# Chunk scores of a bidirectional SSD mixer: masked CB triangles kept in PSUM, time-step weights formed ahead of the exponentials

## The chip, the cores and the metric

The kernel runs on one core of a Trainium2 chip. The metric is device time in microseconds (us) of one execution, as the median of several runs; lower is better. The core's engines are called by the profile's names: PE (TensorE; PEld is its weight load), DVE (VectorE), ACT (ScalarE), POOL (GpSimd) and SP (which only issues DMAs here). A program on one core works out of SBUF and of PSUM, which has eight banks of 128 partitions x 512 float32.

## The reference, cut to what matters

One encoder block on 1024 tokens plus 16 meta tokens, width 1024: an input projection, a gated depthwise convolution, a bidirectional Mamba-2 (SSD) mixer with 4 groups of 8 heads, a gated merge, and a SwiGLU feed-forward part. The change lies in the SSD mixer. It works in chunks of 128 tokens. For a chunk and a direction:

```python
cb = jnp.einsum('bclgn,bcsgn->bcgls', cc, bc)          # one 128x128 matrix per group
lmat = jnp.exp(segsum(adt))                            # one triangle of decays per head
y_diag = jnp.einsum('bcgels,bcsgep->bclgep', cb[:, :, :, None] * lmat, xdt)   # xdt = x * dt
```

So each head's product needs CB, cut to a triangle (lower for the forward direction, upper for the backward one), times the exponentials, times the head's time steps dt. The kernel adds both directions before the product with x.

## The kernel before, in words

The work comes in stages. First an input projection with float32 operands split into a high and a low part, so each product is three matmuls. Then the two convolutions, on DVE with help from ACT and POOL. Then the SSD stage, where the change is. Then the merge and the feed-forward part, which are nearly all matmuls.

**The SSD stage.** Lines 871 to 901 write the order of work out by hand. `backward(0)` runs first: 27 steps that transpose x and B and carry the backward state of group 0. After that a loop visits 32 chunks (4 groups x 8). In each round it walks the string `SEQ` (line 41): `L` loads the next chunk (`load`, line 763), `s` and `t` build its masked decays for heads 0 to 3 and 4 to 7 on POOL (`select`, line 784, instruction on line 760), `S` and `T` turn them into weights (`scores`, line 792), `D`, `O`, `C`, `M`, `V` make the current chunk's outputs, state and norm, and `b`/`e` take a step of the next group's `backward`. The digits are places where background matmuls are let in.

**The background.** `background()` (line 642) is other matmul work that needs no DVE of its own: the two gates' projections (32 groups of 24 matmuls, line 548) and the first half of the SSM output product (16 such groups, line 652). A group accumulates in one PSUM bank with the tag `mm`; ACT copies the bank to SBUF (lines 557 and 658), and a DMA stores it. It is a generator that stops after 6, 15 and 24 matmuls of each group. `step_bg(n)` (line 667) adds `n` to a running sum and takes a step for each whole 1; the weights in `BGW` (line 42) sum to 3.3 for a round.

**Order on the engines.** From line 665 to 902 each matmul is tied behind the one before it, so PE's order is the program's. The other engines' order comes from the framework's scheduler, which sorts ready instructions by program order at build time; each engine then runs its list strictly in that order.

**PSUM.** Line 592 gives the eight banks out as `mm` 2, `tp` 2, `yo` 2, `ss` 1, `yd` 1. After the stage, `ps_ring` (line 593) passes six of them in turn to the later matmuls.

**The weights of a chunk.** `load` computes CB with one matmul into a `tp` bank (line 776), and DVE multiplies it by the two masks into two SBUF tiles, `cbf` (line 778) and `cbb` (line 780). `scores(h4)` adds up the decays on PE into the `ss` bank, ACT takes the exponentials into `e` (line 798), and then, for each of four heads, ACT writes `cbf * dt_f` into `gg` (line 802) and DVE adds `cbb * dt_b` (line 803):

```python
S.activation(out=gg[0][:, h], in_=self.cbf, func=AF.Copy, scale=dt[...])
V.scalar_tensor_tensor(out=gg[0][:, h], in0=self.cbb, scalar=dt[...], in1=gg[0][:, h], op0=ALU.mult, op1=ALU.add)
```

Then DVE multiplies `e` by `gg` (line 805). In the next round `outputs` uses `e` for the `yd` matmuls (line 825), whose result DVE adds to the skip term (line 829). `split_small` (line 691) splits the C matrix on ACT (693) and DVE (694).

Of the kernel before, what the change touches and what calls it, by code (L numbers as in the profile page):

```python
# [8 lines left out]
F32 = mybir.dt.float32  # L9
F32R = mybir.dt.float32r  # L10
AF = mybir.ActivationFunctionType
ALU = mybir.AluOpType
# [3 lines left out]
P = 128  # L16
# [6 lines left out]
NCH = NTT + 1  # L23
DI = 2048
G = 4
HG = 8
# [15 lines left out]
BGW = (0.15, 0.46, 0.29, 0.58, 1.05, 0.14, 0.62, 0.01)  # L42
BG0, BGI = 1.1, 4
ENG = dict(xw="g", xd="v", yy="g", ysz="v", sd="g")
BUFS = dict(xw=4, cc=3, vt=2, s_bl=2, gg=2, e=2, xt=2, btf=5)
LOA, LOB, LOC, LOD = "gg", "vv", "gv", "gv"
EPS = 1e-6
O_VAL, O_GATE, O_Z, O_XS, O_B, O_C, O_DT, O_GC, O_GS = 0, 1024, 2048, 4096, 6144, 6656, 7168, 7232, 8256
# [4 lines left out]
def chunk_span(c):  # L53
    return (0, NM) if c == 0 else (NM + (c - 1) * P, P)
# [3 lines left out]
def tile_hybrid_block(  # L58
# [7 lines left out]
    V, S, GP, PE, SP = nc.vector, nc.scalar, nc.gpsimd, nc.tensor, nc.sync  # L66
    x = x[0]
    out = out[0]
# [126 lines left out]
    def matmul(out_, **kw):  # L195
        tie(PE.matmul(out_, **kw))  # L196

    def transpose(out_, in_, ident_):
        tie(PE.transpose(out_, in_, ident_))  # L199
# [82 lines left out]
    dt = sc.tile([P, NCH, 2 * NH], F32, name="dt")  # L282
# [306 lines left out]

    psB_ctx.close()  # L590
    psp = ctx.enter_context(tc.tile_pool(name="psp", bufs=1, space=PSUM))
    PSB = dict(mm=2, tp=2, yo=2, ss=1, yd=1)
    ps_ring = cycle(("mm", "yo", "ss", "mm", "yo", "yd"))

    def pb(tag):
        return psp.tile([P, 512], F32, name=tag, tag=tag, bufs=PSB[tag])

    def pc():
        return pb(next(ps_ring))

    sd_ctx = ExitStack()
    sd = sd_ctx.enter_context(tc.tile_pool(name="sd", bufs=2))
# [56 lines left out]
            SP.dma_start(out=d_p[i, :, hh * 512:(hh + 1) * 512], in_=pt)  # L659
            yield  # L660

    ps_bg = lambda: pb("mm")
    bg = background()
    bg_acc = [0.0]
    strict[0] = True
# [1 line left out]
    def step_bg(n):  # L667
        bg_acc[0] += n
        while bg_acc[0] >= 1:
            bg_acc[0] -= 1  # L670
            next(bg, None)

    def hbc(t, c, h0, nh, n, w):

        return t[:n, c, h0:h0 + nh].unsqueeze(2).broadcast_to([n, nh, w])
# [3 lines left out]
    def scaled_x(xt, c, h0, n):  # L679
        xw = sd.tile([P, CG], F32, name="xw", bufs=BUFS["xw"])  # L680
        (GP if ENG["xw"] == "g" else V).tensor_tensor(out=v3(xw[:n]), in0=v3(xt[:n]), in1=hbc(wd, c, h0, HG, n, HD), op=ALU.mult)
        return xw
# [8 lines left out]
    def split_small(t):  # L691
        h, l = (sd.tile([P, P], F32R, name=n_, bufs=BUFS["cc"]) for n_ in ("cch", "ccl"))
        S.copy(out=h, in_=t)
        V.tensor_tensor(out=l, in0=t, in1=h.bitcast(F32), op=ALU.subtract)
        return h, l
# [12 lines left out]
    def backward(g):  # L708

        hb = NH + g * HG  # L710
        s_b = None
        for c in range(NCH - 1, -1, -1):
            t0, n = chunk_span(c)
            xc = sd.tile([P, 4, P], F32, name="xc", bufs=3)
            SP.dma_start(out=xc[:, :, :n], in_=d_x[g][:, :, t0:t0 + n])
            bc = sd.tile([P, P], F32, name="bc")
            SP.dma_start(out=bc[:, :n], in_=d_b[g][:, t0:t0 + n])
            ps = pb("tp")
            for j in range(4):
                transpose(ps[:n, j * P:(j + 1) * P], xc[:, j, :n], ident)  # L720
            xt = sd.tile([P, CG], F32, name="xt", bufs=BUFS["xt"])
            S.copy(out=xt[:n], in_=ps[:n])
            SP.dma_start(out=d_xt[g][c, :n], in_=xt[:n])
            yield
            ps = pb("tp")
            transpose(ps[:n, :P], bc[:, :n], ident)
            bt = sd.tile([P, P], F32, name="bt", bufs=BUFS["btf"])
            S.copy(out=bt[:n], in_=ps[:n, :P])
            SP.dma_start(out=d_bt[g][c, :n], in_=bt[:n])
            if c >= 2:  # L730
                xw = scaled_x(xt, c, hb, n)
            yield
            if c >= 2:
                s_b = state_step(s_b, bt, xw, c, hb, n, "s_b")
                SP.dma_start(out=d_sb[g][c - 1], in_=s_b)
            yield
# [3 lines left out]
    def first_state(g):  # L740

        xt = sd.tile([P, CG], F32, name="xt", bufs=BUFS["xt"])
        SP.dma_start(out=xt[:NM], in_=d_xt[g][0, :NM])
        bt = sd.tile([P, P], F32, name="bt", bufs=BUFS["btf"])
        SP.dma_start(out=bt[:NM], in_=d_bt[g][0, :NM])
        xw = scaled_x(xt, 0, g * HG, NM)

        def go():
            state[g] = state_step(None, bt, xw, 0, g * HG, NM, "s_f")
        return go  # L750

    class Chunk:
# [10 lines left out]
        def load(self):  # L763
            g, c = self.g, self.c
            self.first = first_state(g) if c == 1 else None
            t0 = chunk_span(c)[0]
            self.xt = sd.tile([P, CG], F32, name="xt", bufs=BUFS["xt"])
            SP.dma_start(out=self.xt, in_=d_xt[g][c])
            self.bt = sd.tile([P, P], F32, name="bt", bufs=BUFS["btf"])
            SP.dma_start(out=self.bt, in_=d_bt[g][c])  # L770
            bc = sd.tile([P, P], F32, name="bc")
            SP.dma_start(out=bc, in_=d_b[g][:, t0:t0 + P])
            self.cc = sd.tile([P, P], F32, name="cc", bufs=3)
            SP.dma_start(out=self.cc, in_=d_c[g][:, t0:t0 + P])
            ps = pb("tp")
            matmul(ps[:, :P], lhsT=bc, rhs=self.cc, start=True, stop=True)
            self.cbf = sd.tile([P, P], F32, name="cbf")
            V.tensor_tensor(out=self.cbf, in0=ps[:, :P], in1=m_le.bitcast(F32), op=ALU.mult)
            self.cbb = sd.tile([P, P], F32, name="cbb")
            V.tensor_tensor(out=self.cbb, in0=ps[:, :P], in1=m_ge.bitcast(F32), op=ALU.mult)  # L780
            self.e = []
            self.ccs = split_small(self.cc)

        def select(self, h4):
            self.sels = []
            for src in (adh, adl):
                for back in (0, 1):
                    s_ = sd.tile([P, 4, P], F32R, name="sel", bufs=4)
                    self.sel(s_, src.bitcast(F32), (self.hb if back else self.hf) + h4, back)
                    self.sels.append(s_)  # L790

        def scores(self, h4):
            ss = pb("ss")
            for q_, s_ in enumerate(self.sels):
                matmul(ss, lhsT=(u_gt, u_lt)[q_ % 2], rhs=s_.rearrange("p h l -> p (h l)"),
                          start=(q_ == 0), stop=(q_ == 3))
            e = sd.tile([P, 4, P], F32, name="e", bufs=BUFS["e"])
            S.activation(out=e.rearrange("p h l -> p (h l)"), in_=ss, func=AF.Exp)
            gg = [sd.tile([P, 4, P], F32, name="gg", bufs=BUFS["gg"])]
            for h in range(4):  # L800
                hs_ = slice(h4 + h, h4 + h + 1)
                S.activation(out=gg[0][:, h], in_=self.cbf, func=AF.Copy, scale=dt[:, self.c, self.hf:self.hf + HG][:, hs_])  # L802
                V.scalar_tensor_tensor(out=gg[0][:, h], in0=self.cbb, scalar=dt[:, self.c, self.hb:self.hb + HG][:, hs_],  # L803
                                       in1=gg[0][:, h], op0=ALU.mult, op1=ALU.add)
            V.tensor_tensor(out=e, in0=e, in1=gg[0], op=ALU.mult)
            self.e.append(e)

        def outputs(self):
# [60 lines left out]
            SP.dma_start(out=d_vn[g][:, :, i * P:(i + 1) * P], in_=vt)  # L869

    step_bg(BGI)
    for _ in backward(0):
        step_bg(BG0)
    chunks = [Chunk(g, c) for g in range(G) for c in range(1, NCH)]
    NCK = len(chunks)
# [7 lines left out]
    for f in range(NCK + 1):  # L883
        cur = chunks[f] if f < NCK else None
        nxt = chunks[f + 1] if f + 1 < NCK else None
        old = chunks[f - 1] if f else None
        if f % NTT == 0:
            nb = backward(f // NTT + 1) if f // NTT + 1 < G else iter(())
        ahead = lambda: next(nb, None)
        extra = ahead if f % NTT < 2 else (lambda: None)  # L890
        work = dict(
            L=lambda: nxt and nxt.load(), s=lambda: nxt and nxt.select(0), S=lambda: nxt and nxt.scores(0),
            t=lambda: nxt and nxt.select(4), T=lambda: nxt and nxt.scores(4),
            D=lambda: cur and cur.outputs(), O=lambda: cur and cur.off_diag(), C=lambda: cur and cur.carry(),
            M=lambda: cur and cur.norm(), V=lambda: old and old.store(), b=ahead, e=extra)
        for k in SEQ:
            if k in work:
                work[k]()
            else:
                step_bg(BGW[int(k)])  # L900
    step_bg(1000)
    strict[0] = False
    sd_ctx.close()
# [75 lines left out]
    op = load_vn(1)  # L979
# [9 lines left out]
    op = ln_split(0) + ln_split(1)  # L989
# [44 lines left out]
    for b in range(4):  # L1034
        wh, wl = next_w(f"o{b}")
        for i in range(NTT):
            ps = pc()
# [131 lines left out]
```

## Time and profile before

| | |
|---|---|
| median of 3 runs | 2341.51 us (2341.08 to 2342.58) |
| the profiled execution, its own time | 2346.3 us |
| its span, first to last instruction | 2344.1 us |
| PE busy | 2247.3 us (96%) |
| DVE busy | 1445.8 us (62%) |
| ACT busy | 769.1 us (33%) |
| POOL busy | 843.4 us (36%) |
| mean granted TensorE clock | 0.983 of full |

Shares of the whole span mix stages with different limits, so the stage of the change is read alone: it begins with the first score weights at about 785 us of the span, and its last chunk's weights are done at about 1295 us. A matmul's duration in the rows is that of a pipelined instruction: successive matmuls of 512 columns begin 0.23 us apart while each row says 0.39 us. Rows of DVE and ACT overlap by about 0.1 us in the same way.

### The profile page before, as it was taken

Reading aid. Unit: us, or ns where it says so; the run is one execution under the profiler, and the core shown is the slowest. Engines: PE = TensorE matmul, PEld = TensorE weight load, DVE = VectorE, ACT = ScalarE, POOL = GpSimd, SP = SyncE. Lnnn points to the kernel's source line nnn. Section 1 sums busy time; section 2 is a strip of 40 time slices with the busy share of each in tenths; the row PEclk is TensorE's granted clock in tenths of the full one; section 3 lists DMA queues with packets and bytes.
Section 4 is the critical chain, followed back from the end, with each engine's and each line's share of the span. In section 5 each row is a group of like instructions: output and inputs, shape, how many; then the busy total and the mean of one; then the engine's idle time right before and its main releaser. Section 6 shows DMA issues by size and latency. Waiting matters only on the chain.

```text
span 2344.1 us, 31010 instructions
## 1 busy us (share of the span) xinstructions
PE 2247.3 (96%) x12103; PEld 1916.5 (82%) x12103; DVE 1445.8 (62%) x1726; ACT 769.1 (33%) x1385; POOL 843.4 (36%) x730
## 2 busy tenths in 40 slices
PE   8999899999999999888898999999999999999998
PEld 7999899999997666666666778898888888888887
DVE  4398898996771688888999675524233333333236
ACT  6333332323322445445544454214211111111112
POOL 3374654822112576777676241011101101101012
PEclk9999999999999999999999999999999999999999
DMA  4221222233236665656653652421111111111111
GB/s 137 87 72 64 73 76 69 82 104 104 89 102 200 186 198 155 201 155 194 210 167 120 227 177 90 146 66 37 43 47 54 37 54 54 36 54 54 36 54 72
DMA packets 223161, 245.29 MB, mean 105 GB/s; under 512 B 19112, under 2 KB 174360, under 8 KB 223016
## 3 DMA queue, kind: packets, MB, share of 16 engines
q1 hardware_dynamic: 210200, 221.89, 30.6%
q10 hardware_dynamic: 12816, 21.44, 2.5%
q8 instruction: 95, 1.56, 0.3%
q14 instruction: 50, 0.41, 0.1%
HBM read 174.23 MB, written 69.04 MB: 104 GB/s over the span
## 4 chain that ended last, share of the span: by engine, by line
PE 74%; DVE 7%; POOL 6%; issue 4%; DMA 3%; ACT 3%; SPq 0%; POOLq 0%; DVEq 0%; ACTq 0%
PE mm L196 31%; PE yo L196 12%; PE mm L272 6%; PE ss L196 5%; PE yd L196 4%; PE mm L1093 3%; PE yo L1093 3%; DVE gg L803 2%; POOL tap L517 2%; PE ss L1093 2%; PE yd L1093 2%; PE mm L1044 1%; PE yo L1044 1%; POOL wl L139 1%; PE tp L199 1%
## 5 line engine op out<-in xcount | busy, mean ns | idle before, releaser
L139 POOL TENSOR_TENSOR wl<-wraw,wh 128x1024 fp32r<-128x1024 f32 (+1 forms) x103 | 249.9, 2436 | 1116.5 <-ACT wh L138 1116.3
L196 PE MATMUL mm<-hnh,wh 128*128 128x352 f32 (+4 forms) x1248 | 428.0, 343 | 1.4 <-ACT w L275 0.9
L196 PE MATMUL mm<-hnl,wh 128*128 128x352 f32 (+4 forms) x1248 | 421.1, 337 | 0.4 <-DVE hnl L378 0.4
L196 PE MATMUL mm<-hnh,wl 128*128 128x352 f32 (+4 forms) x1248 | 418.7, 335 | 0.0
L138 ACT CAST wh<-wraw 128x1024 fp32r<-128x1024 f32 (+1 forms) x172 | 174.5, 1041 | 403.1 <-PE yd L1093 175.5
L139 DVE TENSOR_TENSOR wl<-wraw,wh 128x1024 fp32r<-128x1024 f32 x69 | 134.4, 1952 | 252.2 <-ACT wh L138 246.5
L478 DVE SCALAR_TENSOR_TENSOR acc<-ap,pr,acc 128x1024 f32<-128x1024 f32 x192 | 247.5, 1289 | 6.3
L196 PEld LDWEIGHTS mm<-hnh,wh 128*128 128x128 f32 x1248 | 235.7, 189 | 15.4 <-issue 2.4
L196 PEld LDWEIGHTS mm<-hnl,wh 128*128 128x128 f32 x1248 | 235.5, 189 | 12.4 <-issue 2.4
L196 PEld LDWEIGHTS mm<-hnh,wl 128*128 128x128 f32 x1248 | 235.4, 189 | 11.3
L196 PE MATMUL mm<-opl,wh 128*128 128x512 f32 x472 | 187.5, 397 | 8.0 <-DVE opl L625 7.9
L196 PE MATMUL mm<-oph,wh 128*128 128x512 f32 x472 | 190.0, 403 | 1.7 <-ACT oph L624 1.6
L803 DVE SCALAR_TENSOR_TENSOR gg<-cbb,dt,gg 128x128 f32<-128x128 f32 x256 | 167.4, 703 | 34.7 <-ACT gg L802 34.5
L196 PE MATMUL mm<-oph,wl 128*128 128x512 f32 x472 | 186.5, 395 | 0.0
L272 PE MATMUL mm<-wh,hnh 128*128 128x256 f32 x512 | 148.5, 291 | 12.2 <-ACT w L275 12.1
L478 DVE SCALAR_TENSOR_TENSOR acc<-xp,pr,acc 128x1040 f32<-128x1040 f32 x120 | 156.6, 1305 | 4.0
L272 PE MATMUL mm<-wl,hnh 128*128 128x256 f32 x512 | 147.6, 289 | 0.0
L272 PE MATMUL mm<-wh,hnl 128*128 128x256 f32 x512 | 147.4, 288 | 0.0
L196 PE MATMUL yo<-oph,wh 128*128 128x512 f32 x352 | 139.0, 395 | 0.0
L196 PE MATMUL yo<-opl,wh 128*128 128x512 f32 x352 | 138.9, 395 | 0.0
L196 PE MATMUL yo<-oph,wl 128*128 128x512 f32 x352 | 138.8, 394 | 0.0
L196 PEld LDWEIGHTS mm<-opl,wh 128*128 128x128 f32 x472 | 88.7, 188 | 32.2 <-DVE opl L625 10.7
(280 smaller groups left out, 4759.6 us busy)
## 6 DMA issues: line engine op xcount, KB each, us to landing
wraw<-in_w_in_dram SPq DMA_DIRECT2D x72, 512.0 KB, 3.7
xc<-d_x SPq DMA_DIRECT2D x64, 256.0 KB, 3.5
wraw<-in_w_gate_dram SPq DMA_DIRECT2D x22, 512.0 KB, 4.2
wraw<-in_w_up_dram SPq DMA_DIRECT2D x22, 512.0 KB, 4.1
wraw<-in_w_down_dram SPq DMA_DIRECT2D x22, 512.0 KB, 3.7
d_x<-xa ACTq DMA_DIRECT2D x16, 520.0 KB, 2.6
d_sz<-w ACTq DMA_DIRECT2D x64, 128.0 KB, 1.8
d_xt<-xt SPq DMA_DIRECT2D x32, 256.0 KB, 3.0
```

Source lines behind the costliest of these rows:

```text
L138: S.copy(out=h3[:, sl], in_=r3)
L139: (V if lo[i] == "v" else GP).tensor_tensor(out=l3[:, sl], in0=r3, in1=h3[:, sl].bitcast(F32), op=ALU.subtract)
L196: tie(PE.matmul(out_, **kw))
L199: tie(PE.transpose(out_, in_, ident_))
L272: PE.matmul(ps[:, :256], lhsT=a[:, sl], rhs=bb[:, k, :], start=(k == 0 and q_ == 0), stop=(k == KC - 1 and q_ == 2))
L478: V.scalar_tensor_tensor(out=out_ if last else acc, in0=sl(k), scalar=w(k), in1=acc, op0=ALU.mult, op1=ALU.add)
L517: GP.tensor_tensor(out=t, in0=t, in1=part, op=ALU.add)
L803: V.scalar_tensor_tensor(out=gg[0][:, h], in0=self.cbb, scalar=dt[:, self.c, self.hb:self.hb + HG][:, hs_], in1=gg[0][:, h], op0=ALU.mult, ...
L1044: PE.matmul(ps[:, :256], lhsT=a[:, sl], rhs=bb[:, k, :], start=(k == 0 and q_ == 0), stop=(k == KC - 1 and q_ == 2))
L1093: PE.matmul(ps, lhsT=a[:, sl], rhs=bb[:, k, t0:t0 + n], start=(k == 0 and q_ == 0), stop=(k == 1 and q_ == 2))
```

## The change

The CB triangles no longer lie in SBUF. A new PSUM bank, `cb`, takes the CB matmul in its columns 0 to 127 and the two masked triangles in columns 128 to 383. The bank is taken from `mm`, which keeps one. The sums `cbf * dt_f + cbb * dt_b` are formed by a new method, `weigh`, for four heads at once: first ACT's four, then DVE's four. It is called at `load` for heads 0 to 3 and at the head of `select(4)` for heads 4 to 7; `scores` only multiplies. There are four `gg` buffers in place of two. The background's bank is now drawn from a ring: `mm`, `ss`, `yd` until the 19th of the 27 steps of `backward(0)`, `mm` alone from there to the end of the chunk loop, and four banks for whatever is left.

```diff
-BUFS = dict(xw=4, cc=3, vt=2, s_bl=2, gg=2, e=2, xt=2, btf=5)
+BUFS = dict(xw=4, cc=3, vt=2, s_bl=2, gg=4, e=2, xt=2, btf=5)
...
-    PSB = dict(mm=2, tp=2, yo=2, ss=1, yd=1)
-    ps_ring = cycle(("mm", "yo", "ss", "mm", "yo", "yd"))
+    PSB = dict(mm=1, tp=2, yo=2, ss=1, yd=1, cb=1)
+    ps_ring = cycle(("mm", "yo", "ss", "cb", "yo", "yd"))
+
+    bg_ring = [cycle(("mm", "ss", "yd"))]
...
-    ps_bg = lambda: pb("mm")
+    ps_bg = lambda: pb(next(bg_ring[0]))
...
-            ps = pb("tp")
+
+            ps = pb("cb")
             matmul(ps[:, :P], lhsT=bc, rhs=self.cc, start=True, stop=True)
-            self.cbf = sd.tile([P, P], F32, name="cbf")
+            self.cbf, self.cbb = ps[:, P:2 * P], ps[:, 2 * P:3 * P]
             V.tensor_tensor(out=self.cbf, in0=ps[:, :P], in1=m_le.bitcast(F32), op=ALU.mult)
-            self.cbb = sd.tile([P, P], F32, name="cbb")
             V.tensor_tensor(out=self.cbb, in0=ps[:, :P], in1=m_ge.bitcast(F32), op=ALU.mult)
-            self.e = []
+            self.e, self.gg = [], []
+            self.weigh(0)
             self.ccs = split_small(self.cc)
+
+        def weigh(self, h4):
+
+            gg = sd.tile([P, 4, P], F32, name="gg", bufs=BUFS["gg"])
+            hs_ = lambda h0, h: dt[:, self.c, h0 + h4 + h:h0 + h4 + h + 1]
+            for h in range(4):
+                S.activation(out=gg[:, h], in_=self.cbf, func=AF.Copy, scale=hs_(self.hf, h))
+            for h in range(4):
+                V.scalar_tensor_tensor(out=gg[:, h], in0=self.cbb, scalar=hs_(self.hb, h), in1=gg[:, h],
+                                       op0=ALU.mult, op1=ALU.add)
+            self.gg.append(gg)
 
         def select(self, h4):
             self.sels = []
+            if h4:
+                self.weigh(h4)
...
             S.activation(out=e.rearrange("p h l -> p (h l)"), in_=ss, func=AF.Exp)
-            gg = [sd.tile([P, 4, P], F32, name="gg", bufs=BUFS["gg"])]
-            for h in range(4):
-                hs_ = slice(h4 + h, h4 + h + 1)
-                S.activation(out=gg[0][:, h], in_=self.cbf, func=AF.Copy, scale=dt[:, self.c, self.hf:self.hf + HG][:, hs_])
-                V.scalar_tensor_tensor(out=gg[0][:, h], in0=self.cbb, scalar=dt[:, self.c, self.hb:self.hb + HG][:, hs_],
-                                       in1=gg[0][:, h], op0=ALU.mult, op1=ALU.add)
-            V.tensor_tensor(out=e, in0=e, in1=gg[0], op=ALU.mult)
+            V.tensor_tensor(out=e, in0=e, in1=self.gg[h4 // 4], op=ALU.mult)
             self.e.append(e)
...
     step_bg(BGI)
-    for _ in backward(0):
+    for n_, _ in enumerate(backward(0)):
+        if n_ == 3 * NCH - 9:
+            bg_ring[0] = cycle(("mm",))
         step_bg(BG0)
...
+    bg_ring[0] = cycle(("mm", "ss", "yd", "cb"))
     step_bg(1000)
```

## Rows read from the trace of the kernel before

**Rows 1.** The page's busy tenths in 40 slices of 58.6 us, three lines.

```profile
DVE  4398898996771688888999675524233333333236
...
POOL 3374654822112576777676241011101101101012
PEclk9999999999999999999999999999999999999999
```

**Rows 2.** Busy us by stretch: PE, PEld, DVE, ACT, POOL, granted clock, DMA share, GB/s.

```profile
690.00:785.00 95.00, 94.53 (x510) 78.14 (x509) 25.79 (x28) 25.50 (x50) 17.98 (x17) 1.00 0.62 191
785.00:1295.00 510.00, 457.19 (x2266) 331.81 (x2265) 455.33 (x708) 254.70 (x621) 363.42 (x440) 0.95 0.58 174
1295.00:1320.00 25.00, 24.07 (x122) 18.50 (x120) 11.78 (x18) 13.03 (x22) 1.49 (x4) 1.00 0.60 177
```

**Rows 3.** Waits of PE, 785 to 1295 us: total us, times, longest us.

```profile
PE yd L196 <- DVE e L805: 21.5, 11, 4.6
PE yo L196 <- DVE y L837: 8.1, 5, 2.9
PE mm L196 <- DVE opl L625: 7.9, 6, 2.4
PE tp L199 <- DVE y L854: 7.6, 9, 1.7
```

**Rows 4.** DVE by line, 785 to 1295 us: busy us, mean ns | idle before.

```profile
L803 DVE SCALAR_TENSOR_TENSOR gg<-cbb,dt,gg 128x128 f32<-128x128 f32 x256 | 167.4, 703 | 34.7 <-ACT gg L802 34.5
L805 DVE TENSOR_TENSOR e<-e,gg 128x512 f32<-128x512 f32 x64 | 54.1, 846 | 1.9 <-ACT e L798 1.1
...
L780 DVE TENSOR_TENSOR cbb<-tp,m_ge 128x128 f32<-128x128 f32 x32 | 8.8, 276 | 0.0
```

**Rows 5.** Single lines of DVE and POOL: duration ns min/median/max, first and last start.

```profile
L803 DVE SCALAR_TENSOR_TENSOR gg<-cbb,dt,gg x256: 332/715/2889, 785.7 to 1293.1; 128x128 f32<-128x128 f32 x128
...
L829 DVE TENSOR_TENSOR xc<-yd,xc x32: 673/677/693, 795.3 to 1300.9; 128x512 f32<-128x512 f32 x32
...
L478 DVE SCALAR_TENSOR_TENSOR acc<-ap,pr,acc x192: 1276/1290/1291, 123.4 to 489.2; 128x1024 f32<-128x1024 f32 x192
...
L805 DVE TENSOR_TENSOR e<-e,gg x64: 672/679/1547, 790.4 to 1294.7; 128x512 f32<-128x512 f32 x64
...
L760 POOL TENSOR_SCALAR_AFFINE_SELECT sel<-adh x128: 626/682/3242, 713.9 to 1287.6; 128x512 fp32r<-128x512 f32 x128
```

**Rows 6.** PE in order of time, at three ends of background groups.

```profile
784.27 0.39 PE L196 MATMUL mm<-hnh,wl 128*128 128x512 f32 x1
784.50 0.38 PE L196 MATMUL tp<-cc,bc 128*128 128x128 f32 x2
784.64 0.47 PE L196 MATMUL mm<-hnh,wh 128*128 128x512 f32 x1
...
1134.48 0.39 PE L196 MATMUL mm<-oph,wh 128*128 128x512 f32 x1
...
1307.25 0.39 PE L196 MATMUL mm<-oph,wl 128*128 128x512 f32 x1
1307.48 0.39 PE L196 MATMUL mm<-oph,wh 128*128 128x512 f32 x1
```

**Rows 7.** ACT in order of time: the copies that follow those three groups.

```profile
784.74 0.59 ACT L557 COPY w<-mm 128x512 f32<-128x512 f32 x1 [3.99 <-PE mm L196]
...
1139.21 0.57 ACT L658 COPY w<-mm 128x512 f32<-128x512 f32 x1
...
1309.17 0.57 ACT L658 COPY w<-mm 128x512 f32<-128x512 f32 x1
```

**Rows 8.** Waits of ACT, 785 to 1295 us: total us, times, longest us.

```profile
ACT sz L858 <- DVE y L855: 134.2, 30, 8.5
```

**Rows 9.** ACT by line, 785 to 1295 us: busy us, mean ns | idle before.

```profile
L802 ACT ACTIVATE gg<-cbf,dt 128x128 f32<-128x128 f32 x256 | 83.4, 390 | 0.2
```

## Prediction

> **What bounds the kernel now.** I read the page's slices first: DVE is at nine tenths in only two places, the convolutions and slices 15 to 22, and in the second POOL is busy too [rows 1]. Then the stretches. Before the stage of the change PE is busy 94.5 of 95 us, after it 24.1 of 25. In the stage PE is busy 457 of 510 us, so idle 53, while DVE is busy 455 (89%) [rows 2]. The granted clock there is 0.95 where the neighbours have 1.00. With levels of 2.4 and 1.2 GHz that is a tenth of the stage at the lower one, or 0.05 x 510 = 25 us of matmul work lost. So what a change here can win at most is 53 + 25 = 78 us, and the stretches to both sides can give nothing.
>
> The waits of PE say whom it waits for: DVE, 21.5 + 8.1 + 7.9 + 7.6 = 45.1 of the 53 us; the largest is the `yd` matmuls waiting for the weighted exponentials (line 805) [rows 3]. DVE's costliest group is line 803, the 256 sums of the two triangles, 167 of its 455 us [rows 4]. Its shortest instance takes 332 ns, the median 715 [rows 5]: something doubles it. POOL's masks take 682 ns each beside it [rows 5].
>
> **The change part by part.**
>
> *Line 803 reads one triangle from PSUM.* No row shows this instruction with one input there, but nearby ones bound it. Line 829 (PSUM and SBUF in, 512 columns) lies between 673 and 693 ns through the same stage, and line 478, the same operation with a per-partition scalar, between 1276 and 1291 ns for 1024 columns while POOL was busy, whereas line 805 with both inputs in SBUF reaches 1547 ns against a shortest 672 [rows 1, 5]. So an input from PSUM frees a DVE instruction of POOL's traffic. From 677 ns for 512 columns and 276 for 128 [rows 4, 5] a column costs 1.04 ns; 128 columns of line 478's form are then 1290 - 896 x 1.04 = 358 ns. Saving: 256 x (703 - 358) = 88 us of DVE. The ends are 0 (the mean stays 703) and 256 x (703 - 332) = 95 us; I take 88, since lines 829 and 478 are the same kind. Given back: POOL's reads now fall on the other two-SBUF instructions; line 805 averages 846 ns against 672 [rows 4, 5], 64 x 0.17 = 11 us, and I allow it once more, +11. DVE's load falls from 455 to about 378 us, 74% of the stage.
>
> *The sums are formed ahead of the exponentials.* Between an exponential and its product DVE now runs four sums, 4 x 0.70 = 2.8 us; afterwards none. The `yd` waits average 21.5 / 11 = 2.0 us [rows 3], less than that. They should go: -21 us of PE idle time (ends 0 and -21.5).
>
> *DVE's backlog.* The other three waits, 23.6 us, are for instructions that stand in DVE's list behind others. DVE's free share goes from 11% to 26%, so I take a bit over half off: -13 us (ends 0 and -23.6).
>
> *The background loses a bank.* With one `mm` bank a group can't begin until ACT has copied the last one out. I went through the ends of the 37 groups from 784 to 1308 us (the first, the worst and the last stand in [rows 6, 7]). At 13 of them the next group begins under 0.4 us later. With ACT's copies where they are, PE would be held at 17 ends: 0.7 us at the first (785.33 against 784.64), 5.3 at the worst (1139.78 against 1134.48), 2.3 at the last; together 32 us. If each copy followed its group as promptly as at the first, it would be 10 us. These are the ends. ACT's copies are late because ACT stands 134 us waiting for line 855 of DVE [rows 8], and DVE gets faster; so I take a value near the low end, +13. In the last nine steps of `backward(0)` some three more groups end, at most 0.8 us each: +2. Those steps have nothing else to win, as PE is full there [rows 2].
>
> *The turns in the new bank.* `cbf` and `cbb` share a bank, and the code runs ACT's four and then DVE's four. If the two engines may not overlap there, each set waits for four ACT instructions. In the rows of before ACT and DVE work on `gg` side by side, and DVE already idles 34.5 us for ACT there [rows 4]. No row shows two engines in one bank. Below, nothing, as the sums lie ahead of their use; above, 64 sets x 4 x 0.30 us (390 ns less the 0.1 us of overlap) = 77 us of DVE waiting, of which 34.5 are paid now. With 378 us of load DVE has room for 43 more (421 of 510), so I put +2 on the path. Masking into PSUM (64 instructions, 276 ns) and ACT reading from PSUM (390 ns now, [rows 9]) I cost at nothing: DVE's and ACT's slack (ACT is idle half the stage) hides them; without it, a change of 50 ns would be 3 and 13 us. The CB matmul now waits for the previous chunk's last sums; these are issued half a round, some 8 us (510 / 32 / 2), earlier, so nothing. The DMAs are the same; SP, POOL and the later stages are not touched.
>
> *The clock.* Idle time of PE goes from 53 to 53 - 21 - 13 + 13 + 2 = 34 us. I let the 25 us lost to the lower clock fall with it: 25 x 34 / 53 = 16, so -9 (ends 0 and -25).
>
> Sum: -21 - 13 + 13 + 2 + 2 - 9 = -26 us. It is made against the profiled execution, 2346.3 us (span 2344.1), which lies 4.8 us above the median of the runs, 2341.5. So 2320 there, and **2315.5** for the median.
>
> The Trainium skill bears on the turns ("PSUM — Partial Sum Buffer", section "PSUM bank collisions raise a hardware error"): two engines must not touch one bank on the same partitions at once, two readers included, and the hardware does not arbitrate, so software has to keep them apart. By that rule the turns are certain; by the rows alone they are only likely. It speaks against this change, and its result is the second rival.
>
> **The rivals.** A measurement of this kernel tells about 0.2% (4.7 us) from no change.
>
> *The single background bank decides; slower.* Place: the ends of groups in the chunk loop. For it: 32 us with ACT's present timing, and one bad end costs 5.3. Against it: ACT's lateness comes mostly from DVE. If DVE's backlog stays as it is, only the `yd` waits go: -21 + 32 + 2 = +13 of idle time, and the clock loses 25 x 13 / 53 = 6 more: +19, **2360**. It decides as soon as the holds at the group ends pass the 34 us that PE stops waiting for DVE. Chance 0.14.
>
> *The turns eat the freed time; no change.* DVE gains 88 and gives back 11, but waits up to 77 us for ACT's fours, so its list advances as slowly as before: 88 - 11 - 77 = 0, **2341**. For it: DVE's idle time before line 803 is already ACT's. Against it: other DVE work can be put into these gaps. Chance 0.12.
>
> *The change does not do what it says.* The sums stay at 703 ns, since `gg` and the scalar still come from SBUF. Then -21 by the earlier sums, +15 by the bank: -6 or nearer zero, **2338**. Lines 829 and 478 speak against it. Chance 0.06.
>
> *PE is fed fully.* All 45 us of DVE waits and most of the clock go: -45 - 22 + 12 = -55, **2286**. Against it: some waits also follow DMAs and ACT. Chance 0.10.
>
> **How the numbers follow.** The forecast has the rest, 0.58; its own range is 2300 to 2332. The whole range runs from 2288, which takes in all of it and most of the full-feed case, to 2348, which takes in the two cases of no change and a mild form of the slower one; about 0.16 is left out. Faster by over 0.2%: 0.57 of the forecast's, the full feed, nothing of the others: 0.67. Within 0.2%: 0.18. Slower: 0.15.
>
> **What would show it.** Right: line 803 near 360 ns with a narrow spread; DVE busy near 75% of the stage; the `yd` wait for line 805 all but gone; the stage some 25 us shorter, with a granted clock of 0.96 to 0.98; a new wait of PE's `mm` for ACT's copies (lines 557 and 658 shift) of 10 to 20 us. Wrong: that wait at 30 us or more; or DVE idle before line 803 at 70 us or more with the other waits of PE unchanged; or line 803 still at a median of 700 ns. A gain outside the SSD stage would not be explained by any of this.

## The result, and the profile after

The changed kernel takes 2317.81 us (median of 4 runs, 2316.69 to 2318.26) beside 2342.05 us for the kernel before in the same session: a ratio of 0.9894, 95% interval 0.9879 to 0.9909, so 24 us faster. The forecast was 2315.5. The profiled execution took 2316.69 us with a span of 2314.9, which is 29 us less than that of before.

The stretches of the changed kernel first (busy us of PE, PEld, DVE, ACT, POOL, then granted clock, DMA share, GB/s), to be held against [rows 2]:

```profile
690.00:785.00 95.00, 93.96 (x501) 77.12 (x500) 24.98 (x26) 24.68 (x48) 17.98 (x17) 1.00 0.61 188
785.00:1275.00 490.00, 453.81 (x2310) 330.45 (x2309) 398.15 (x715) 253.42 (x628) 364.99 (x442) 0.98 0.62 184
1275.00:1300.00 25.00, 24.57 (x112) 19.61 (x111) 10.76 (x16) 13.13 (x22) 0.74 (x2) 1.00 0.65 200
```

PE's idle time in the stage is 490 - 454 = 36 us where it was 53, the granted clock 0.98 where it was 0.95, and DVE is busy 81% of the stage where it was 89%. Then the stage's own instructions, the weights of ACT and DVE and the product (duration ns min/median/max, first and last start):

```profile
L792 ACT ACTIVATE gg<-cb,dt x256: 344/368/395, 786.0 to 1262.4; 128x128 f32<-128x128 f32 x128
L794 DVE SCALAR_TENSOR_TENSOR gg<-cb,dt,gg x256: 332/341/354, 787.2 to 1264.1; 128x128 f32<-128x128 f32 x128
L815 DVE TENSOR_TENSOR e<-e,gg x64: 676/1076/2703, 789.1 to 1267.1; 128x512 f32<-128x512 f32 x64
```

The 256 sums now lie between 332 and 354 ns; before, their shortest was 332 and their median 715 [rows 5]. The first to the last product takes 478 us (789.1 to 1267.1) where it took 504 (790.4 to 1294.7, [rows 5]): 26 of the 29 us are in this stage. But the product, whose two inputs are in SBUF, got slower, from a median of 679 to 1076 ns. The groups of DVE show who else did (780 to 1290 us; busy us, mean ns | idle before):

```profile
L794 DVE SCALAR_TENSOR_TENSOR gg<-cb,dt,gg 128x128 f32<-128x128 f32 x256 | 71.8, 342 | 40.3 <-ACT gg L792 40.2
L815 DVE TENSOR_TENSOR e<-e,gg 128x512 f32<-128x512 f32 x64 | 66.9, 1046 | 14.5 <-ACT e L814 13.8
...
L839 DVE TENSOR_TENSOR xc<-yd,xc 128x512 f32<-128x512 f32 x32 | 21.9, 683 | 3.0 <-PE yd L196 2.7
```

The sums cost 72 us where they cost 167 [rows 4], the product 67 where it cost 54. Line 839, one input in PSUM, has hardly moved (a mean of 683 ns where line 829, its counterpart, took 679). Last, the waits of PE in the stage (total us, times, longest us), against [rows 3]:

```profile
PE mm L196 <- ACT w L557: 15.7, 10, 4.4
PE mm L196 <- ACT w L660: 10.7, 8, 4.5
PE mm L196 <- DVE opl L627: 2.6, 3, 1.2
PE mm L196 <- ACT oph L626: 2.2, 1, 2.2
PE yd L196 <- DVE e L815: 1.7, 3, 1.0
```

Before, DVE held PE for 45 us and ACT's copies of `mm` for nothing. Now DVE holds it for some 5 us and the copies for 26. The worst hold is worth reading in order of time. PE's rows:

```profile
1118.59 0.39 PE L196 MATMUL mm<-oph,wl 128*128 128x512 f32 x1
1123.44 0.80 PE L196 MATMUL mm<-oph,wh 128*128 128x512 f32 x1 [4.47 <-ACT w L660]
```

and ACT's in the same stretch:

```profile
1118.25 0.73 ACT L870 ACTIVATE y<-y,rs 128x512 f32<-128x512 f32 x1 [2.49 <-POOL rs L119]
1118.89 1.32 ACT L626 ACTIVATE oph<-wraw,pr 128x512 fp32r<-128x512 f32 x2
1120.11 1.11 ACT L792 ACTIVATE gg<-cb,dt 128x128 f32<-128x128 f32 x4
1121.11 0.59 ACT L724 COPY xt<-tp 128x512 f32<-128x512 f32 x1
1121.58 0.62 ACT L814 ACTIVATE e<-ss 128x512 f32<-128x512 f32 x1
1122.07 0.64 ACT L689 CAST sbh<-s_bl 128x512 fp32r<-128x512 f32 x1
1122.57 0.33 ACT L695 CAST cch<-cc 128x128 fp32r<-128x128 f32 x1
1122.77 0.62 ACT L660 COPY w<-mm 128x512 f32<-128x512 f32 x1
```

The group's last matmul begins at 1118.6, and the copy that frees its bank begins at 1122.8: ACT, back from a wait of 2.5 us for POOL's short step of the norm (line 119), first runs through seven groups of other work. This is the rule and not the exception. Worked out from the trace over all 18 holds, 26.6 us pass between the end of a group and the start of its copy, and ACT is idle in only 5 of them. In the run with two `mm` banks (e6) PE no longer waits for these copies.

### The profile page after: what moved, and what is told of

It reads as the page before. It is cut to its first block, busy times and chain, and to the rows that moved or that the text cites. A ratio compares the mean times of both kernels' runs of the same rounds, so it can differ in the third digit from the quotient of the medians.

```text
span 2314.9 us, 31003 instructions
## 1 busy us (share of the span) xinstructions
PE 2234.7 (97%) x12103; PEld 1908.0 (82%) x12103; DVE 1382.8 (60%) x1726; ACT 764.1 (33%) x1385; POOL 842.9 (36%) x730
## 4 chain that ended last, share of the span: by engine, by line
PE 46%; DVE 3%; DMA 2%; ACT 2%; POOL 1%; issue 1%; SPq 0%; POOLq 0%; DVEq 0%; ACTq 0%
PE yo L196 11%; PE mm L196 8%; PE ss L196 4%; PE yd L196 4%; PE cb L196 4%; PE yo L1106 3%; PE ss L1106 2%; PE cb L1106 2%; PE yd L1106 2%; PE mm L1106 1%; PE yo L1057 1%; DMA wraw<-d_vn 1%; PE cb L1057 1%; PE ss L1057 1%; PE yd L1057 1%
## 5 line engine op out<-in xcount | busy, mean ns | idle before, releaser
L196 PE MATMUL mm<-hnh,wh 128*128 128x352 f32 (+4 forms) x1208 | 411.0, 340 | 17.7 <-ACT w L557 16.3
L196 PE MATMUL mm<-hnl,wh 128*128 128x352 f32 (+4 forms) x1208 | 405.8, 336 | 0.4 <-DVE hnl L378 0.4
L196 PE MATMUL mm<-hnh,wl 128*128 128x352 f32 (+4 forms) x1208 | 403.5, 334 | 0.0
L196 PEld LDWEIGHTS mm<-hnh,wh 128*128 128x128 f32 x1208 | 228.3, 189 | 32.7 <-ACT w L557 20.6
L196 PEld LDWEIGHTS mm<-hnl,wh 128*128 128x128 f32 x1208 | 228.2, 189 | 9.8 <-issue 1.2
L196 PE MATMUL mm<-oph,wh 128*128 128x512 f32 x344 | 139.7, 406 | 12.8 <-ACT w L660 10.7
L196 PE MATMUL mm<-opl,wh 128*128 128x512 f32 x344 | 137.2, 399 | 2.6 <-DVE opl L627 2.6
L196 PE MATMUL mm<-oph,wl 128*128 128x512 f32 x344 | 136.9, 398 | 0.0
L762 POOL TENSOR_SCALAR_AFFINE_SELECT sel<-adh 128x512 fp32r<-128x512 f32 x128 | 96.7, 775 | 68.8 <-ACT wh L138 41.6
L272 PEld LDWEIGHTS mm<-wh,hnh 128*128 128x128 f32 x512 | 100.5, 197 | 13.5 <-ACT w L275 13.4
```

What stands on the lines that cost most here:

```text
L272: PE.matmul(ps[:, :256], lhsT=a[:, sl], rhs=bb[:, k, :], start=(k == 0 and q_ == 0), stop=(k == KC - 1 and q_ == 2))
L762: GP.affine_select(out=dst, in_=hbc(src, self.c, h0, 4, P, P), pattern=[[0, 4], [-1 if back else 1, P]], compare_op=ALU.is_ge, fill=0.0, b ...
```

## The experiments

Each kernel was run 4 to 11 times beside the kernel before (e11 once). Ratios are to the kernel before; the changed kernel stands at 0.9894 (0.9879 to 0.9909). e5 to e8 were timed together in one session, and e5 turned out to run the very same instructions in the same order as the changed kernel. Its 0.9876 (0.9859 to 0.9892) therefore shows what a repeat can differ by, some 4 us of 2342, and e6 to e8 are held against both. Theory A: the PSUM operand of the 256 sums relieves DVE and carries most of the gain. Theory B: forming the sums ahead of the exponentials does.

**e1: the sums behind the exponential again, the triangles still in PSUM.**

```diff
-            self.weigh(0)
...
-            if h4:
-                self.weigh(h4)
...
             S.activation(out=e.rearrange("p h l -> p (h l)"), in_=ss, func=AF.Exp)
+            self.weigh(h4)
             V.tensor_tensor(out=e, in0=e, in1=self.gg[h4 // 4], op=ALU.mult)
```

> As the changed kernel, but the four sums of a set come after the exponential again, ahead of the product, as in the kernel before. Theory A (the PSUM operand relieves DVE, and that is most of the gain; the early place gives the rest): a sum stays at 340 ns, DVE stays near 80% of the stage, PE's wait of the yd matmuls for the product is back at 5 to 12 us, total 2320 to 2330. Theory B (the early place is what pays, the relief of DVE alone is off the path): yd wait 15 to 22 us and the lost bank on top, total 2340 to 2360.

2317.71 us, ratio 0.990 (0.9884 to 0.9915): the same as the changed kernel. A sum stays at 341 ns, and PE has no wait of the `yd` matmuls for the product at all in the stage. Better than A expected: the early place gives nothing that can be measured once DVE is relieved.

**e2: the early place alone**, triangles in SBUF, banks as before.

```diff
+            self.weigh(0)
             self.ccs = split_small(self.cc)
...
+            if h4:
+                self.weigh(h4)
...
-            V.tensor_tensor(out=e, in0=e, in1=gg[0], op=ALU.mult)
+            V.tensor_tensor(out=e, in0=e, in1=self.gg[h4 // 4], op=ALU.mult)
```

> As the kernel before (triangles in SBUF, two background banks, CB in a tp bank), but the sums are formed in fours at load and at select(4), with four gg buffers. Theory A: a sum stays near 700 ns and DVE at 88% or more; the yd wait falls under 8 us, but PE's other waits for DVE stay or grow (15 to 30 us); total 2325 to 2338. Theory B: the yd wait goes and nothing comes in its place; with no bank lost the total is 2300 to 2318, at or under the changed kernel.

2346.86 us, ratio 1.0022 (1.0013 to 1.003): slower by 5 us, and neither theory's number. The durations of the weights, then PE's largest waits in the stage:

```profile
L792 DVE SCALAR_TENSOR_TENSOR gg<-cbb,dt,gg x256: 334/712/2482, 784.0 to 1294.2; 128x128 f32<-128x128 f32 x128
```

```profile
PE yd L196 <- DVE e L813: 19.7, 11, 3.5
PE mm L196 <- DVE opl L625: 11.7, 4, 6.9
```

The `yd` wait I meant to remove this way is there, 19.7 us of 21.5. The product was late because DVE's whole list was, not because the sums stood right ahead of it. The trace of the kernel before says so too. Of the four sums of a set, a mean of only 1.5 start after the set's exponential has ended, and all four do so in 9 of the 64 sets: the build's order had already put most of them ahead. In e2 the mean is 1.0, so there was little to move. B falls.

**e3: the banks alone**, everything else as before.

```diff
-    PSB = dict(mm=2, tp=2, yo=2, ss=1, yd=1)
-    ps_ring = cycle(("mm", "yo", "ss", "mm", "yo", "yd"))
+    PSB = dict(mm=1, tp=2, yo=2, ss=1, yd=1, cb=1)
+    ps_ring = cycle(("mm", "yo", "ss", "cb", "yo", "yd"))
+    bg_ring = [cycle(("mm", "ss", "yd"))]
```

> As the kernel before, with only the banks dealt out as in the changed kernel (one mm bank in the chunk loop, the cb bank left empty until the later stages, the ring of the background the same). Prediction's bounds: PE waits 10 to 32 us for the copies of mm (lines 557 and 658 shift), total slower by 10 to 40, 2352 to 2382. Rival (the scheduler puts ACT's copies earlier, or the holds only move PE's waits for DVE): within 5 us of 2342.

2350.63 us, ratio 1.0036 (1.0024 to 1.0049): 9 us slower, just under the expected range. PE's waits in the stage:

```profile
PE mm L196 <- ACT w L557: 15.0, 10, 3.9
PE mm L196 <- ACT w L660: 9.5, 4, 4.1
PE yd L196 <- DVE e L807: 7.8, 7, 3.0
```

The hold is 24.5 us, but the `yd` wait fell from 21.5 to 7.8, which fits DVE catching up while PE was held at `mm`. By the total, some 16 us of the hold replaced waits that PE would have had anyway.

**e4: the forward triangle back in SBUF**, so ACT no longer uses the `cb` bank.

```diff
-            self.cbf, self.cbb = ps[:, P:2 * P], ps[:, 2 * P:3 * P]
+            self.cbf = sd.tile([P, P], F32, name="cbf")
+            self.cbb = ps[:, 2 * P:3 * P]
```

> As the changed kernel, but the forward triangle lies in SBUF, so only DVE (and PE) uses the cb bank. Theory of turns on the path: ACT's and DVE's fours may overlap, DVE's wait for ACT before the sums falls from 40 us to under 25 and ACT's wait for the sums from 9.5 to 0, total 2304 to 2313. Theory A (turns lie beside the path): the same waits fall, or other ones replace them, and the total stays at 2314 to 2322.

2311.82 us, ratio 0.9875 (0.9861 to 0.9888); the interval overlaps that of the changed kernel. DVE's wait for ACT at the sums falls from 40.2 to 31.4 us; ACT's wait for DVE's sums, 9.5 us in the changed kernel, is gone, though ACT's reads take 388 ns from SBUF where they took 368 from PSUM. The total lies in the range of turns on the path, but the threshold of 25 us was missed, and the gain of some 4 us is no larger than that of e5, which changed no instruction. That the turns cost time is not shown.

**e5: the background's copies given priority** in the build's order of ACT.

```diff
-                S.copy(out=gt, in_=ps)
+                with tc.high_priority():
+                    S.copy(out=gt, in_=ps)
```

> As the changed kernel, with the background's two copies out of the mm bank (lines 557 and 660) given priority in the build's order of ACT. Theory H (PE's new wait is ACT being busy with other ready work): PE's mm wait for ACT falls from 26 us to under 15 and the total to 2303 to 2313. Rival (ACT stands blocked on DVE or POOL when the group ends, so the order helps little): wait 20 us or more, total 2314 to 2322.

2314.94 us, ratio 0.9876 (0.9859 to 0.9892). The edit did not do what it was meant to. In the two traces every engine runs the same instructions in the same order, all 1385 of ACT among them. At the worst hold the copy still begins behind the same other work (two of the rows between are shown):

```profile
1114.92 0.72 ACT L872 ACTIVATE y<-y,rs 128x512 f32<-128x512 f32 x1 [2.23 <-POOL rs L119]
...
1118.72 0.64 ACT L691 CAST sbh<-s_bl 128x512 fp32r<-128x512 f32 x1
1119.23 0.33 ACT L697 CAST cch<-cc 128x128 fp32r<-128x128 f32 x1
1119.43 0.62 ACT L662 COPY w<-mm 128x512 f32<-128x512 f32 x1
```

So PE's wait stayed at 15.4 + 11.5 = 26.9 us because nothing was moved, and neither theory H nor its rival was tested. That ACT is busy for some four fifths of the delay before a copy speaks for H; whether an earlier copy would pay is open.

**e6: the bank taken from `tp` in place of `mm`.**

```diff
-    PSB = dict(mm=1, tp=2, yo=2, ss=1, yd=1, cb=1)
+    PSB = dict(mm=2, tp=1, yo=2, ss=1, yd=1, cb=1)
```

> As the changed kernel, with the lost bank taken from tp (transposes) in place of mm: mm 2, tp 1. If the lost background bank costs what PE's wait for it shows: that wait goes from 26 us to under 8, and if transposes bear one bank, total 2296 to 2310. Rival (the transposes then wait for their bank): PE's tp waits rise from about 1 us to 15 or more, total 2314 or slower.

2306.61 us, ratio 0.9839 (0.9824 to 0.9854): clear of the changed kernel by 0.55%, 13 us, and of its repeat e5 by 8 us. PE's largest waits in the stage:

```profile
PE tp L199 <- ACT vt L878: 14.4, 10, 3.5
PE tp L199 <- ACT bt L730: 7.9, 10, 3.0
```

The `mm` hold is gone and 22 us of `tp` holds came in its place, so each side was right about its wait; by total it is still a gain. All waits of PE in the stage together fell from 36 to 29 us, and the granted clock of the stretch from 785 to 1275 us rose from 0.98 to 0.99, which fits that gain.

**e7: the exponential stays in PSUM**, so the product too has only one input in SBUF.

```diff
-            S.activation(out=e.rearrange("p h l -> p (h l)"), in_=ss, func=AF.Exp)
-            V.tensor_tensor(out=e, in0=e, in1=self.gg[h4 // 4], op=ALU.mult)
+            S.activation(out=ss, in_=ss, func=AF.Exp)
+            V.tensor_tensor(out=e, in0=ss.rearrange("p (h l) -> p h l", l=P), in1=self.gg[h4 // 4], op=ALU.mult)
```

> As the changed kernel, but ACT leaves the exponential in the ss bank, so the product of line 815 has one input in PSUM. Theory A (two SBUF inputs are what POOL slows): the product falls from a mean of 1046 ns to 670 to 700, its longest from 2703 to under 720, DVE busy in the stage falls by 15 to 25 us or other two-input lines take some of it. Total: 2314 to 2322 if DVE no longer sets PE's pace (its waits for DVE are under 7 us already), 2300 to 2311 if it still does; slower than 2322 if the ss bank, held longer, makes PE wait.

2310.36 us, ratio 0.9854 (0.9839 to 0.9869): 0.4% under the changed kernel, with intervals apart, but only 0.2% (4.6 us) under its repeat e5, where the intervals overlap. The product's durations:

```profile
L815 DVE TENSOR_TENSOR e<-ss,gg x64: 673/682/693, 789.3 to 1262.4; 128x512 f32<-128x512 f32 x64
```

and the waits of PE it left in the stage:

```profile
PE mm L196 <- ACT w L557: 11.3, 8, 4.4
PE ss L196 <- DVE e L815: 9.5, 7, 3.6
PE mm L196 <- ACT w L660: 8.7, 6, 3.6
```

The median falls from 1076 to 682 ns, and DVE is busy 373 us of the stretch (785 to 1275 us) where it was 398. The total lies in the range given for DVE still setting PE's pace. The path may lead through ACT, whose wait for line 865 falls from 92.6 to 71.4 us and the `mm` hold with it, from 26 to 20; that is a reading of the waits, not shown by itself.

**e8: the backward triangle alone in PSUM.** The banks of e3, and one tile moved; the forward triangle, the sums' place, their order head by head and the two `gg` buffers are those of before.

```diff
-            ps = pb("tp")
+            ps = pb("cb")
...
-            self.cbb = sd.tile([P, P], F32, name="cbb")
+            self.cbb = ps[:, P:2 * P]
```

> As the kernel with the banks alone moved (e3), plus one thing: the CB matmul goes to the cb bank and the backward triangle stays there, so the 256 sums have one input in PSUM. Forward triangle in SBUF, sums late, head by head, two gg buffers, all as before. Theory A (this one operand carries the whole gain): sums at 340 ns, total 2308 to 2320. Rival (the fours, the early place or the gg buffers are needed as well): 2325 or slower.

2309.32 us, ratio 0.985 (0.9835 to 0.9864): better than the changed kernel, whose other parts together cost it some 10 us (0.0044 x 2342), or 6 us by its repeat e5. The sums' durations:

```profile
L805 DVE SCALAR_TENSOR_TENSOR gg<-cb,dt,gg x256: 333/342/354, 783.1 to 1256.3; 128x128 f32<-128x128 f32 x128
```

**e12: e8 with its triangle back in SBUF**, the CB matmul still in the `cb` bank.

```diff
-            self.cbb = ps[:, P:2 * P]
+            self.cbb = sd.tile([P, P], F32, name="cbb")
```

> As e8, but the backward triangle goes back to SBUF: only the CB matmul uses the cb bank. It differs from e8 in nothing but where line 780 writes and line 805 reads. Theory A (the operand of the sums is the gain): sums back near 700 ns, total 2342 to 2353, as e3. Rival (a good part of e8's gain is CB leaving the tp banks): 2335 or faster.

2351.56 us, ratio 1.0037 (1.0023 to 1.005), as in e3. The sums are back where they were:

```profile
L805 DVE SCALAR_TENSOR_TENSOR gg<-cbb,dt,gg x256: 332/712/2882, 784.6 to 1298.3; 128x128 f32<-128x128 f32 x128
```

So CB's leaving the `tp` banks gives nothing, and the place of one operand is worth 0.0187 x 2342 = 44 us: theory A, shown by an edit of a single line.

**e9 and e10: the winners together.** e9 is e8 with the bank taken from `tp` (the diff of e6); e10 adds the exponential in PSUM (the diff of e7).

> As e8 (only the backward triangle in PSUM, the rest as before), with the bank taken from tp as in e6: mm 2, tp 1. If the two gains are separate and add (e8 about 10 us under the changed kernel, e6 about 13): 2292 to 2301 beside a kernel before of 2342. Rival (both win the same time, PE being near full): 2302 to 2310, with PE idle 25 us or more in the stage from tp waits.

> As e9, and the exponential stays in the ss bank, so the product too has one input in PSUM (e7). If DVE's relief still pays: 3 to 8 us under e9. Rival (PE waits for the ss bank, as the 9.5 us in e7, and DVE no longer limits): within 2 us of e9 or slower.

e9: 2302.53 us, ratio 0.9827 (0.9814 to 0.9841), some 5 us under e8 with intervals that overlap, and not the sum of the two gains: the rival's range, though PE's `tp` waits are 19.4 us and not the 25 that the rival named. e10: 2295.40 us, ratio 0.9803 (0.9789 to 0.9817), 7 us under e9 with intervals that just touch, as expected of DVE's relief still paying. It beats both kernels, the one before by 2.0% and the changed one by 0.9% (0.7% by e5). PE's largest waits left in the stage of e10:

```profile
PE tp L199 <- ACT vt L870: 5.8, 8, 1.6
PE ss L196 <- ACT bt L730: 4.0, 2, 2.2
PE ss L196 <- DVE e L807: 3.4, 3, 1.6
```

**e11: POOL's part.** The kernel before with half of POOL's masks; it leaves out the low halves of the decays, and half of the score matmuls with them.

```diff
-            for src in (adh, adl):
+            for src in (adh,):
```

> The kernel before, leaving out the low halves of the decays: POOL makes two masks in place of four for each set and PE two matmuls in place of four, so the time itself is not to be compared. If POOL's reading is what lengthens the 256 sums with both inputs in SBUF: their mean falls from 703 ns to between 450 and 600, with the shortest still near 332, and the product's mean from 846 to under 800. If it is something else (DVE's own second read, ACT or PE beside it): 680 to 720, unchanged.

The mean of the sums is 641 ns, between the two ranges. The line's durations:

```profile
L803 DVE SCALAR_TENSOR_TENSOR gg<-cbb,dt,gg x256: 334/527/2483, 783.8 to 1247.4; 128x128 f32<-128x128 f32 x128
```

The median falls from 715 to 527 ns and the mean of the product from 846 to 769. With half the masks POOL is still busy 272 of 490 us, with other work that reads SBUF, so the run by itself leaves open how much of the lengthening is POOL's. The traces settle it when each sum is held against what POOL runs at the time. In the kernel before, the 44 sums during which POOL runs nothing take 332 to 350 ns, and the other 212 a mean of 779 (40 of them stay under 400). Two sums beside a mask, then the two that follow when POOL has stopped (POOL's masks end at 885.4 us, its next instruction begins at 887.4):

```profile
L803 DVE SCALAR_TENSOR_TENSOR gg<-cbb,dt,gg x2: 718/776/834, 884.1 to 884.9; 128x128 f32<-128x128 f32 x2
L803 DVE SCALAR_TENSOR_TENSOR gg<-cbb,dt,gg x2: 332/336/340, 885.5 to 886.4; 128x128 f32<-128x128 f32 x2
```

```profile
884.15 1.28 POOL L760 TENSOR_SCALAR_AFFINE_SELECT sel<-adl 128x512 fp32r<-128x512 f32 x2
887.38 1.65 POOL L844 TENSOR_TENSOR y<-y,y 128x512 f32<-128x512 f32 x1 [1.95 <-DVE y L843]
```

In e11 there are 84 sums without POOL, at 335 to 355 ns, and the other 172 still average 787: fewer masks meant fewer sums beside POOL, not shorter ones. In the changed kernel 235 of the 256 sums run beside POOL and none takes more than 354 ns. So the lengthening comes only while POOL runs, and one input in PSUM removes it.

## Why the prediction was right, and where its steps were not

*Line 803 from PSUM* was the step that mattered, and it was priced right: 358 ns forecast, 342 measured, so 256 x (703 - 342) = 92 us against 88. Lines 829 and 478, the rows it was worked out from, did predict a line that no row showed. (One reading beside it was loose: in [rows 1] DVE stands at eight tenths in slices 15 to 19 and at nine only in 20 to 22. The working went by the stretches and does not rest on it.)

*Given back* was too small in kind: I allowed the product once more its own excess, 11 us, and it took 64 x 0.20 = 13, but other two-SBUF lines lengthened too. The split of line 694, now 696, went from a mean of 482 to 673 ns. DVE was busy 398 us in place of 378, 81% of a shorter stage, not 74% of the old one.

*The sums ahead of the exponentials, -21 us:* this step failed. The wait went, but for another reason. Its premise, that DVE runs four sums between an exponential and its product, holds for 9 of 64 sets; the mean is 1.5 sums, and 1.1 in the changed kernel. e1 keeps the gain without the early place; e2 keeps the early place and has the wait at 19.7 us. The `yd` wait belonged to *DVE's backlog*, the next step, which I had priced at -13 for the other three waits: all four together fell from 45 to under 5 us. The error was to price a wait by the instructions that stood directly ahead of the releaser, when the releaser's engine was late throughout. Together the two steps were put at -34 and measured -40; the sum came near because what the one had too much the other had too little, and that is luck.

*The background's bank, +13 and +2:* 26 us in place of 15, inside the bounds of 10 to 32. This term was too small. I leaned on ACT becoming prompter once DVE was faster. Its wait for line 855 did fall, from 134 to 93 us, but little of it falls where it would delay a copy: ACT is idle in only 5 of the 26.6 us between the ends of these groups and their copies, and busy with other work in the rest. How much of that work was itself late from earlier waits is open. Taken alone the bank costs 9 us of total for 24.5 us of wait, since it replaces other waits as long as DVE is the slower engine; with DVE relieved more of it may be paid, and e6 gives 8 to 13 us back.

*The turns:* they exist. ACT waits 9.5 us, 26 times, for DVE's sums, a wait that the kernel before could not have, and DVE's idle time ahead of the sums rose from 34.7 to 40.3 us, far from the 77 of the second rival. By the rule of the Trainium skill ("PSUM — Partial Sum Buffer", section "PSUM bank collisions raise a hardware error") the two may not share the bank at once; the trace agrees that they take turns: none of ACT's reads of line 792 overlaps in time with a sum of line 794, while their counterparts in the kernel before ran side by side for 61 us. What happens without turns no run here shows, nor that the +2 was right.

*The clock, -9:* 0.95 to 0.98, so 25 us of lost work become 0.02 x 490 = 10: -15. The loss did not fall in proportion to PE's idle time, as the step had it: the idle time fell by a third (53 to 36 us), the loss by more than half.

With the measured terms: -40 (DVE's waits) + 26 (bank) - 15 (clock) = -29 us, and the two profiled executions differ by 29.6. So close an agreement is partly chance, as the clock's two figures are rounded and only 26 us lie between the first and the last product. The forecast of -26 came near for a like reason: the waits for DVE (-6), the bank (+11) and the clock (-6) each missed, and the misses offset each other.

The rival of the single bank wanted the holds at the group ends to pass the 34 us that PE would stop waiting for DVE; they came to 26 against 40. That the sums stay at 703 ns is refuted by their durations. PE was not fed fully: 26 of the 36 us that it is still idle are the new holds.

## What to carry to other kernels

Where DVE lags beside a busy POOL, hold the shortest against the median duration of its lines: a wide gap on lines with two SBUF inputs and none on lines with one input in PSUM points to both the loss and the remedy. Then split the instances of such a line by whether POOL runs beside them. Short instructions lost most here: the 128-column sums went from 332 to a mean of 703 ns, the 512-column product from 672 to 846. Move the one operand that is needed and nothing else, and find the PSUM bank for it by trying which of its users misses it least. Hold a run's order of instructions against that of the kernel that it was made from, before reading anything from its time: e5 had changed nothing. A wait of PE names the instruction that came last, not why its engine was late; before pricing it, ask whether that engine's whole list is behind.

## What the runs showed of the hardware that was not expected

Traffic of POOL that no longer lengthens one DVE line lengthens some of the others. With the sums out of its way, the product's mean rose from 846 to 1046 ns though its two inputs still lay in SBUF, and fell to 684 once one of them was in PSUM (e7). The splits of lines 694 (482 to 673) and 688 (912 to 1072) rose too, while line 855 stayed at 950 and line 625 fell from 977 to 912. A sum with both inputs in SBUF takes 332 to 350 ns while POOL runs nothing, and a mean of 779 beside POOL. ACT reads a 128x128 triangle with a scale in 368 ns from PSUM and 389 from SBUF (medians); DVE's masking took a mean of 290 and 294 ns into PSUM where it took 280 and 276 into SBUF.
